# Four pairs of K tiles by seven products in some gate chunks, and a seven-product block prepared in another order

## The chip, the cores and the metric

The kernel runs on one core of a Trainium2 chip. The metric is the device time of one execution in microseconds (us). The engines are named as the profile names them: PE (TensorE, matrix products), PEld (its weight loads), DVE (VectorE), ACT (ScalarE), POOL (GpSimd, which here mostly issues DMAs) and SP (SyncE, which issues most DMAs). Each engine takes its instructions strictly in the order in which they stand in its own program.

## The reference, cut to what matters

Two layers act on a residual stream of 256 tokens by 2048 features: an SSD (Mamba-2) mixer in the first, differential attention in the second, and behind each a SwiGLU feed-forward stage. The change is in the two feed-forward stages alone:

```python
def swiglu(h, w_gate, w_up, w_down):
    return (jax.nn.silu(h @ w_gate) * (h @ w_up)) @ w_down
# h: 256 x 2048; w_gate, w_up: 2048 x 5632; w_down: 5632 x 2048, all float32
```

## The kernel before

**Products.** Every float32 operand is split into a rounded part "hi" and the remainder "lo", both in the format that PE reads, and a product of two tiles is three matmuls (hi by hi, hi by lo, lo by hi), each with 512 columns. Weights arrive by DMA as raw float32 blocks. ACT makes hi as a rounded copy (line 133) and DVE makes lo by a subtraction (line 134); the pair is called a prep. Four buffers of hi and four of lo rotate, so the hi of one prep must wait until PE has done with the prep four places earlier.

**Pairs.** `pair` (line 218) makes two neighbouring output chunks of 512 columns for both halves of the tokens (128 rows each) at once. It walks over blocks, and each block is one pair of K tiles: two K tiles by two chunks of weights, 128 x 2048 numbers. An ordinary block takes eight products (24 matmuls) and one prep. A block whose number is in the list `seven` is done by Winograd's form of Strassen's scheme with seven products (21 matmuls): sums of weight tiles stand against sums ("forms") of the activation tiles. For it the weights need a sum of two quarters that a DMA on the POOL queue adds in memory (line 247), a prep of three quarters, three additions on DVE (lines 261 to 263) and a second prep of four quarters, so it takes two hi and two lo buffers. The forms of an activation pair are made by `make_form` (line 822) from the split activations, each in one of four buffers of 128 x 1024 numbers ("xr").

**Order.** Each feed-forward stage has three parts (`PARTS`). In a part, for each pair of chunks, the gate pair is followed by the up pair, and behind the chunks of a part stand the pairs of the down projection that use them. With eight blocks in a gate or up pair, blocks 2, 4 and 6 are done by seven. The part numbers below are 1 to 3; parts 2 and 3 have two gate and two up pairs each (chunks 2 and 3, 4 and 5; 6 and 7, 8 and 9). The forms of blocks 2, 4 and 6 are kept in DRAM, since their buffers serve the down projection's forms at the end of a part, and are read back over the POOL queue (line 927) when parts 2 and 3 begin. Work put off with `later(k, ...)` is emitted k half-blocks on: so, within the second gate pair of a part, the transposes and splits of the activations of the up pair before it ("act pieces", lines 284 and 285) and a form for the down projection. A scheduler then sets the order of each engine's instructions. Five raw buffers take turns, and SP and POOL queue their DMAs ahead as buffers come free.

Of the kernel before, what the change touches and what calls it, by code (L numbers as in the profile page):

```python
# [16 lines left out]
P = 128  # L17
# [15 lines left out]
SEVEN = (2, 4, 6)  # L33

# [7 lines left out]
def trunk_kernel(ctx, tc, x_rows, x_cols, vec_cols, vec64, post_rows, lam_rows,  # L42
# [177 lines left out]
    def pair(blocks, stat, seven, form, done):  # L220
# [20 lines left out]
        for kp, src in enumerate(blocks):  # L241
# [17 lines left out]
            hi, lo = prep(raw[:, 1:4])  # L259

            nc.vector.tensor_tensor(raw[:, 2], raw[:, 2], raw[:, 0], op=ALU.add)
            nc.vector.tensor_tensor(raw[:, 3], raw[:, 3], raw[:, 2], op=ALU.add)
            nc.vector.tensor_tensor(raw[:, 1], raw[:, 2], raw[:, 1], op=ALU.subtract)  # L263
            sh, sl = prep(raw)
            mm("p1", stat(kp, 0, 0), hi[:, 1], lo[:, 1], last)
            mm((0, 0), stat(kp, 1, 0), hi[:, 2], lo[:, 2], False)
            mm((0, 1), form(kp, 3), hi[:, 0], lo[:, 0], False)
            tick()
            mm("p6", form(kp, 2), sh[:, 2], sl[:, 2], last)
            mm("p5", form(kp, 0), sh[:, 1], sl[:, 1], last)  # L270
            mm("p7", form(kp, 1), sh[:, 0], sl[:, 0], last)
            mm((1, 0), stat(kp, 1, 1), sh[:, 3], sl[:, 3], False)
# [547 lines left out]
    def make_form(dct, key, stat, t512, keep=None):  # L820
# [3 lines left out]
        for t in range(NT):  # L824
            for j in range(2):
                hi, lo = stat(key, j, t)
                nc.vector.tensor_tensor(xf[:, t, j], hi.bitcast(F32), lo.bitcast(F32), op=ALU.add)
# [30 lines left out]
    def ffn(wg, wu, wd, step, final):  # L858
# [17 lines left out]
        def kg_stat(kg, j, t):  # L876
            hi, lo = lookup(acts, (t, kg // 2))
            return hi[:, kg % 2 * 2 + j], lo[:, kg % 2 * 2 + j]
# [258 lines left out]
```

## Time and profile before

| what | value |
|---|---|
| median of 3 runs (lowest, highest) | 2540.77 us (2540.26, 2540.88) |
| the profiled execution: its time, the span of its instructions | 2539.5 us, 2537.7 us |
| PE busy | 2517.8 us, 99% |
| DVE busy | 1902.6 us, 75% |
| ACT busy | 1364.7 us, 54% |
| POOL busy | 222.4 us, 9% |
| granted TensorE clock, mean | 0.998 |

PE is busy nearly throughout, but that is a mean over stages, and PE's share says nothing on how little ahead of it the engines are that feed it. For this the timeline of DVE and ACT is set against PE's at the blocks in question: what matters is when the lo of a block ends and when PE first needs it.

### The profile page before, as it was taken

To read this page: it belongs to the slowest core of one execution; us is meant where nothing else is said; L and a number is where in the kernel's file an instruction comes from. 1 tells how busy PE (TensorE), PEld (TensorE's weight loads), DVE (VectorE), ACT (ScalarE), POOL (GpSimd) and SP (SyncE) were. 2 spreads that over 40 slices of the span, in tenths; PEclk is the share of its full clock that TensorE was granted. 3 is DMA by queue.
4 is the path that set the end of the run, shared out by engine and by line. 5 is a ranking of instruction groups with operands and counts; after the bars stand their busy time and mean duration, and the time that the engine had idled before them with its cause. 6 is when DMAs were issued, how large, how long until landed. Compare 5 with 4: busy or idle time off the path is not lost.

```text
span 2537.7 us, 31211 instructions
## 1 busy us (share of the span) xinstructions
PE 2517.8 (99%) x11866; PEld 2072.2 (82%) x11866; DVE 1902.6 (75%) x2274; ACT 1364.7 (54%) x1655; POOL 222.4 (9%) x214
## 2 busy tenths in 40 slices
PE   9999999999999999999999999999999999999998
PEld 8877888788888888888888888887888888888886
DVE  6777547777687888977887765566688889878985
ACT  5767556666565454544454654455655454535453
POOL 0111000110110000001001100001100000010002
PEclk9999999999999999999999999999999999999999
DMA  7555555455776776778677544544666966786673
GB/s 287 190 169 182 189 191 198 166 183 177 254 260 210 253 238 210 236 231 243 210 237 246 189 150 166 183 151 156 241 223 201 294 216 208 235 262 213 205 252 146
DMA packets 141366, 536.16 MB, mean 211 GB/s; under 512 B 14176, under 2 KB 30880, under 8 KB 114208
## 3 DMA queue, kind: packets, MB, share of 16 engines
q1 hardware_dynamic: 125584, 502.91, 57.3%
q0 software_dynamic: 15264, 30.94, 6.5%
q8 instruction: 93, 1.52, 0.2%
q14 instruction: 57, 0.47, 0.0%
q10 hardware_dynamic: 368, 0.32, 0.0%
HBM read 516.22 MB, written 17.89 MB: 210 GB/s over the span
## 4 chain that ended last, share of the span: by engine, by line
PE 93%; DVE 2%; ACT 1%; issue 1%; DMA 1%; POOL 0%; SPq 0%; DVEq 0%; ACTq 0%; POOLq 0%
PE acc L238 38%; PE acc L187 34%; PE cp L238 8%; PE acc L212 5%; PE acc L214 2%; DVE lo L134 1%; PE sc L1013 1%; DMA mt<-acum_d 1%; PE pt_f L291 1%; ACT hi L133 1%; PE py L568 1%; PE ptx L661 0%; PE po L1049 0%; PE pc L475 0%; PE pp L1040 0%
## 5 line engine op out<-in xcount | busy, mean ns | idle before, releaser
L134 DVE TENSOR_TENSOR lo<-raw,hi 128x2048 fp32r<-128x2048 f32 (+2 forms) x451 | 848.6, 1888 | 362.4 <-ACT hi L133 353.2
L133 ACT CAST hi<-raw 128x2048 fp32r<-128x2048 f32 (+2 forms) x451 | 699.8, 1557 | 593.9 <-DVE raw L263 195.4
L238 PE MATMUL acc<-hi,xT 128*128 128x512 f32 x1840 | 589.2, 390 | 0.0
L187 PE MATMUL acc<-hi,xT 128*128 128x512 f32 x1792 | 588.9, 399 | 0.0
L238 PEld LDWEIGHTS acc<-hi,xT 128*128 128x128 f32 x1840 | 345.3, 188 | 71.5
L187 PEld LDWEIGHTS acc<-hi,xT 128*128 128x128 f32 x1792 | 335.9, 188 | 73.4 <-issue 4.9
L238 PE MATMUL acc<-lo,xT 128*128 128x512 f32 x920 | 358.1, 389 | 0.0
L187 PE MATMUL acc<-lo,xT 128*128 128x512 f32 x896 | 352.1, 393 | 1.1 <-DVE lo L134 1.1
L133 ACT CAST hi<-rawm 128x2048 fp32r<-128x2048 f32 (+1 forms) x115 | 207.8, 1807 | 173.4 <-DVE rawm L263 108.3
L134 DVE TENSOR_TENSOR lo<-rawm,hi 128x2048 fp32r<-128x2048 f32 (+1 forms) x115 | 248.0, 2157 | 69.9 <-ACT hi L133 66.1
L238 PEld LDWEIGHTS acc<-lo,xT 128*128 128x128 f32 x920 | 172.7, 188 | 35.5
L187 PEld LDWEIGHTS acc<-lo,xT 128*128 128x128 f32 x896 | 169.0, 189 | 38.0 <-DVE lo L134 3.6
L238 PE MATMUL acc<-hi,ah_f 128*128 128x512 f32 x468 | 183.1, 391 | 0.0
L238 PE MATMUL acc<-hi,al_f 128*128 128x512 f32 x468 | 182.1, 389 | 0.0
L238 PE MATMUL acc<-lo,ah_f 128*128 128x512 f32 x468 | 182.1, 389 | 0.0
L212 PE MATMUL acc<-xT,hi 128*128 128x512 f32 x512 | 179.8, 397 | 0.0
L238 PE MATMUL cp<-hi,ff 128*128 128x512 f32 x468 | 156.9, 389 | 0.0
L214 PE MATMUL acc<-xT,lo 128*128 128x256 f32 x512 | 142.6, 280 | 0.0
L138 DVE SCALAR_TENSOR_TENSOR lo<-raw,cols,hi 128x512 fp32r<-128x512 f32 x128 | 92.5, 767 | 57.2 <-ACT hi L137 56.9
L137 ACT ACTIVATE hi<-raw,cols 128x512 fp32r<-128x512 f32 x128 | 84.8, 715 | 58.9 <-PE acc L187 41.4
L212 PEld LDWEIGHTS acc<-xT,hi 128*128 128x128 f32 x512 | 96.1, 188 | 22.6
L238 PEld LDWEIGHTS acc<-hi,al_f 128*128 128x128 f32 x468 | 87.8, 188 | 18.4
(279 smaller groups left out, 3470.4 us busy)
## 6 DMA issues: line engine op xcount, KB each, us to landing
raw<-in_w_zxbc_dram SPq DMA_DIRECT2D x77, 1024.0 KB, 4.8
raw<-in_w_d_dram SPq DMA_DIRECT2D x98, 512.0 KB, 5.9
raw<-in_w_g_dram SPq DMA_DIRECT2D x96, 512.0 KB, 5.9
raw<-in_w_u_dram SPq DMA_DIRECT2D x96, 512.0 KB, 5.8
raw<-in_w_qkv_dram SPq DMA_DIRECT2D x48, 1024.0 KB, 4.8
raw<-in_w_so_dram SPq DMA_DIRECT2D x32, 1024.0 KB, 4.8
rawm<-in_w_g_dram SPq DMA_DIRECT2D x64, 512.0 KB, 5.8
rawm<-in_w_u_dram SPq DMA_DIRECT2D x64, 512.0 KB, 6.0
```

What stands on the lines that cost most here:

```text
L133: nc.scalar.copy(hi, raw)
L134: nc.vector.tensor_tensor(lo, raw, hi.bitcast(F32), op=ALU.subtract)
L137: nc.scalar.activation(hi[:, j], raw[:, j], AF.Copy, scale=scale[j])
L138: nc.vector.scalar_tensor_tensor(lo[:, j], raw[:, j], scale[j], hi[:, j].bitcast(F32), op0=ALU.mult, op1=ALU.subtract)
L187: nc.tensor.matmul(acc[t], a, b[:, j], start=(i == 0 and j == 0 and q == 0), stop=(i == last and j == 1 and q == 2))
L212: nc.tensor.matmul(acc[ct], hi[:, j, cs], x.rearrange("p a s -> p (a s)"), start=(i == 0 and j == 0), stop=False)
L214: nc.tensor.matmul(acc[ct][:, :S], lo[:, j, cs], x[:, 0], start=False, stop=(i == last and j == 1))
L238: nc.tensor.matmul(acc[k], a, b, start=first and q == 0, stop=last and q == 2)
L291: nc.tensor.transpose(pt[:, j], src[:, j * P:(j + 1) * P], ident)
L568: nc.tensor.matmul(py[e * 64:(e + 1) * 64, a], xd[c][:, 2 * a + e], mts[c][:, 2 * a + e], start=True, stop=True)
L1013: nc.tensor.matmul(sc[c][:, h], qT[cp, h % 2, ts], kT[cp, h % 2, :nk * P], start=True, stop=True)
```

## The change

A fourth block, block 3, is done by seven products in the gate pairs of parts 2 and 3 (four pairs in each layer), so that there blocks 2, 3 and 4 are sevens one behind the other, then an ordinary block 5, then block 6. The up pairs, part 1 and the down pairs keep their lists. Block 3 needs its own form, which is made and kept beside the others (the order of making is now 3, 2, 4, 6) and read back with them. The read-backs of 4 and 6 are put off by one and by five half-blocks.

The seven-product block itself is also written anew, in all places where it stands (86 blocks against 78 before). Its first prep now covers all four quarters, with the DMA's sum among them, and so waits for that DMA. The second prep is taken apart: three rounded copies of one quarter each on ACT, between the three additions on DVE, and two subtractions (two quarters, then one). The product of the DMA's sum moves from the second half of the block to its first. `make_form` takes two additions of 256 columns in place of four of 128, and one put-off form moves from six half-blocks to eight.

```diff
+SEVEN_G = (2, 3, 4, 6)
+
+SEVEN_F = (3, 2, 4, 6)
...
             last = kp == seven[-1]
-            hi, lo = prep(raw[:, 1:4])
-
+            hi, lo = prep(raw)
+            sh = hl[0].tile([P, 3, 512], F32R, tag="hi", name=f"sh{seq[0]}")
+            sl = hl[0].tile([P, 3, 512], F32R, tag="lo", name=f"sl{seq[0]}")
             nc.vector.tensor_tensor(raw[:, 2], raw[:, 2], raw[:, 0], op=ALU.add)
+            nc.scalar.copy(sh[:, 1], raw[:, 2])
+            nc.vector.tensor_tensor(raw[:, 1], raw[:, 2], raw[:, 1], op=ALU.subtract)
+            nc.scalar.copy(sh[:, 0], raw[:, 1])
             nc.vector.tensor_tensor(raw[:, 3], raw[:, 3], raw[:, 2], op=ALU.add)
-            nc.vector.tensor_tensor(raw[:, 1], raw[:, 2], raw[:, 1], op=ALU.subtract)
-            sh, sl = prep(raw)
-            mm("p1", stat(kp, 0, 0), hi[:, 1], lo[:, 1], last)
-            mm((0, 0), stat(kp, 1, 0), hi[:, 2], lo[:, 2], False)
-            mm((0, 1), form(kp, 3), hi[:, 0], lo[:, 0], False)
+            nc.scalar.copy(sh[:, 2], raw[:, 3])
+            nc.vector.tensor_tensor(sl[:, 0:2], raw[:, 1:3], sh[:, 0:2].bitcast(F32), op=ALU.subtract)
+            nc.vector.tensor_tensor(sl[:, 2], raw[:, 3], sh[:, 2].bitcast(F32), op=ALU.subtract)
+            mm("p1", stat(kp, 0, 0), hi[:, 2], lo[:, 2], last)
+            mm((0, 0), stat(kp, 1, 0), hi[:, 3], lo[:, 3], False)
+            mm((0, 1), form(kp, 3), hi[:, 1], lo[:, 1], False)
+            mm("p7", form(kp, 1), hi[:, 0], lo[:, 0], last)
             tick()
-            mm("p6", form(kp, 2), sh[:, 2], sl[:, 2], last)
-            mm("p5", form(kp, 0), sh[:, 1], sl[:, 1], last)
-            mm("p7", form(kp, 1), sh[:, 0], sl[:, 0], last)
-            mm((1, 0), stat(kp, 1, 1), sh[:, 3], sl[:, 3], False)
+            mm("p6", form(kp, 2), sh[:, 1], sl[:, 1], last)
+            mm("p5", form(kp, 0), sh[:, 0], sl[:, 0], last)
+            mm((1, 0), stat(kp, 1, 1), sh[:, 2], sl[:, 2], False)
...
-            for j in range(2):
-                hi, lo = stat(key, j, t)
-                nc.vector.tensor_tensor(xf[:, t, j], hi.bitcast(F32), lo.bitcast(F32), op=ALU.add)
+            hi, lo = stat(key, t)
+            nc.vector.tensor_tensor(xf[:, t], hi.bitcast(F32), lo.bitcast(F32), op=ALU.add)
...
-        for k, kp in enumerate(SEVEN):
+        for k, kp in enumerate(SEVEN_F):
...
-                for kp in SEVEN:
+                def reload(kp):
                     forms[kp] = xr_tile("ff", (P, 4, 2, P), F32R)
                     nc.gpsimd.dma_start(forms[kp].rearrange("p f h q -> p (f h q)"), keep[kp])
+                forms.clear()
+                for k, kp in zip((0, 0, 1, 5), SEVEN_F):
+                    if k:
+                        later(k, lambda kp=kp: reload(kp))
+                    else:
+                        reload(kp)
...
-                        form_later(6, two[0][0])
-                    pair(twos(wg, c), kp_stat, SEVEN, form, g_done(c // 2))
+                        form_later(8, two[0][0])
+                    pair(twos(wg, c), kp_stat, SEVEN_G if pi else SEVEN, form, g_done(c // 2))
```

The engines' orders follow from the scheduler. Three places matter below. In the rows, "hi" and "lo" are the parts of a first prep (or, before, of either prep), "sh" and "sl" those of the second one in the changed kernel, "raw" and "rawm" the weight blocks, "ff" a form; the number behind the name tells buffers apart.

ACT, second gate pair of part 2 in the first feed-forward stage, from block 2 on, before:

```order
L133 CAST hi282_8336<-raw_8325 128x2048
L284 CAST ff_8375<-f_8366 128x4x128
L133 CAST hi283_8381<-rawm_8378 128x2048
L133 CAST hi284_8413<-raw_8409 128x1536
L133 CAST hi285_8420<-raw_8409 128x2048
L133 CAST hi286_8448<-raw_8445 128x2048
L133 CAST hi287_8480<-rawm_8476 128x1536
L133 CAST hi288_8487<-rawm_8476 128x2048
```

The same engine and place in the changed kernel:

```order
L269 CAST sh267_8391<-raw_8383 128x512
L137 CAST hi267_8430<-rawm_8426 128x2048
L271 CAST sh267_8391<-raw_8383 128x512
L273 CAST sh267_8391<-raw_8383 128x512
L269 CAST sh268_8434<-rawm_8426 128x512
L137 CAST hi268_8480<-raw_8476 128x2048
L271 CAST sh268_8434<-rawm_8426 128x512
L273 CAST sh268_8434<-rawm_8426 128x512
L295 CAST ff_8473<-f_8466 128x4x128
L269 CAST sh269_8484<-raw_8476 128x512
L137 CAST hi269_8518<-raw_8515 128x2048
L271 CAST sh269_8484<-raw_8476 128x512
```

Where one cast of four quarters stood for the second prep, three casts of one quarter stand now, and the whole cast of the next block's weights has come between the first and the second of them. So it is in 70 of the 86 sevens; in 12 the three stand together, and in 4 the next block's cast stands behind the second.

DVE at the same place, before (blocks 4 and 5, then the first lo of block 6):

```order
L134 TENSOR_TENSOR lo284_8414<-raw_8409,hi284_8413 128x1536
L261 TENSOR_TENSOR raw_8409<-raw_8409 128x512
L262 TENSOR_TENSOR raw_8409<-raw_8409 128x512
L263 TENSOR_TENSOR raw_8409<-raw_8409 128x512
L134 TENSOR_TENSOR lo285_8421<-raw_8409,hi285_8420 128x2048
L134 TENSOR_TENSOR lo286_8449<-raw_8445,hi286_8448 128x2048
L134 TENSOR_TENSOR lo287_8481<-rawm_8476,hi287_8480 128x1536
```

And now (block 3, then the first lo of block 4):

```order
L138 TENSOR_TENSOR lo267_8431<-rawm_8426,hi267_8430 128x2048
L268 TENSOR_TENSOR rawm_8426<-rawm_8426 128x512
L270 TENSOR_TENSOR rawm_8426<-rawm_8426 128x512
L272 TENSOR_TENSOR rawm_8426<-rawm_8426 128x512
L274 TENSOR_TENSOR sl268_8435<-rawm_8426,sh268_8434 128x1024
L275 TENSOR_TENSOR sl268_8435<-rawm_8426,sh268_8434 128x512
L138 TENSOR_TENSOR lo268_8481<-raw_8476,hi268_8480 128x2048
```

The subtraction of two quarters (line 274) stands behind ACT's second copy (line 271), and the next block's lo stands behind both subtractions; the ordinary block that lay between two sevens is gone here.

ACT in the first gate pair of part 2, blocks 2 and 3, in the changed kernel:

```order
L137 CAST hi250_7747<-rawm_7743 128x2048
L269 CAST sh251_7751<-rawm_7743 128x512
L271 CAST sh251_7751<-rawm_7743 128x512
L137 CAST hi251_7792<-raw_7788 128x2048
L273 CAST sh251_7751<-rawm_7743 128x512
L269 CAST sh252_7796<-raw_7788 128x512
L271 CAST sh252_7796<-raw_7788 128x512
L273 CAST sh252_7796<-raw_7788 128x512
L137 CAST hi252_7831<-rawm_7827 128x2048
```

Here, in the first two sevens of the pair, no cast of the next block stands ahead of the second copy.

More of the change, by code (lines that the diff above doesn't have):

```diff
@@ L874, in kp_stat, with kp_both, kg_both @@
             return x_stat(2 * kp + j, t)
-        def kg_stat(kg, j, t):
+        def kp_both(kp, t):
+            sl = slice(t * P, (t + 1) * P)
+            ks = slice(kp % 2 * 2, kp % 2 * 2 + 2)
+            return xT_hi[kp // 2][:, ks, sl], xT_lo[kp // 2][:, ks, sl]
+        def kg_both(kg, t):
             hi, lo = lookup(acts, (t, kg // 2))
-            return hi[:, kg % 2 * 2 + j], lo[:, kg % 2 * 2 + j]
+            return hi[:, kg % 2 * 2:kg % 2 * 2 + 2], lo[:, kg % 2 * 2:kg % 2 * 2 + 2]
         def form(kp, f):
@@ L911, in ffn @@
                 nc.sync.dma_start(xr_d[t][h].rearrange("p (e k) -> p e k", e=2), xr_of[(t, h)])
-        for k, kp in enumerate(SEVEN):
+        for k, kp in enumerate(SEVEN_F):
             keep[kp] = dramp.tile([P, 8 * P], F32, name=f"form{step}_{kp}")
-            later(1 + 3 * k, lambda kp=kp: make_form(forms, kp, kp_stat, t512, keep[kp]))
+            later(1 + 3 * k, lambda kp=kp: make_form(forms, kp, kp_both, t512, keep[kp]))
         mv([wu[10, k] for k in range(4)], u_stat, u_evac, LAG2)
         def form_later(k, kg):
-            later(k, lambda: make_form(dforms, kg, kg_stat, t512))
+            later(k, lambda: make_form(dforms, kg, kg_both, t512))
         md = [dramp.tile([P, D], F32, name=f"md{step}_{t}") for t in range(NT)]
```

## The prediction

> **What bounds the kernel now.** The page comes first: its busy shares and the last two lines on the chain of waits.
>
> ```profile
> PE 2517.8 (99%) x11866; PEld 2072.2 (82%) x11866; DVE 1902.6 (75%) x2274; ACT 1364.7 (54%) x1655; POOL 222.4 (9%) x214
> PE 93%; DVE 2%; ACT 1%; issue 1%; DMA 1%; POOL 0%; SPq 0%; DVEq 0%; ACTq 0%; POOLq 0%
> ```
>
> By these PE bounds all, and fewer matmuls would be less time. But the shares are means. So the second view is busy time by stretches, for the eight gate pairs that the change touches, in pairs of lines: the first and the second gate pair of part 2, then of part 3, then the same in the second layer (columns: stretch; its length; PE, PEld, DVE, ACT, POOL busy; granted clock; DMA share; GB/s).
>
> ```profile
> 898.10:939.50 41.40, 41.40 (x184) 34.28 (x183) 33.73 (x29) 20.05 (x13) 1.73 (x2) 1.00 0.75 235
> 980.90:1024.40 43.50, 43.45 (x199) 35.62 (x198) 38.71 (x45) 22.16 (x18) 2.58 (x3) 1.00 0.59 184
> 1150.90:1192.30 41.40, 41.40 (x184) 34.31 (x183) 30.99 (x25) 19.93 (x12) 5.79 (x7) 1.00 0.80 235
> 1233.60:1277.20 43.60, 43.58 (x200) 35.67 (x199) 38.81 (x45) 21.91 (x17) 2.59 (x3) 1.00 0.61 191
> 2010.40:2051.60 41.20, 41.20 (x183) 34.15 (x182) 33.52 (x28) 19.54 (x12) 2.64 (x3) 1.00 0.77 245
> 2092.90:2136.40 43.50, 43.49 (x199) 35.65 (x198) 38.72 (x45) 21.04 (x17) 2.62 (x3) 1.00 0.61 195
> 2263.10:2304.40 41.30, 41.30 (x184) 34.20 (x183) 30.41 (x26) 18.92 (x12) 6.18 (x7) 1.00 0.81 236
> 2345.60:2389.10 43.50, 43.49 (x199) 35.66 (x198) 38.71 (x45) 20.72 (x17) 2.62 (x3) 1.00 0.61 196
> ```
>
> The second pairs ("heavy", 43.5 us) carry 16 transposes, the act pieces and a form besides, and DVE works 38.7 us of 43.5; in the first ("light", 41.3 us) it works 30 to 34. The third view, the timeline of DVE and of PE in the first heavy pair, tells what DVE does with the rest (blocks 4, 5 and 6):
>
> ```profile
> 999.55 1.75 DVE L134 TENSOR_TENSOR lo<-raw,hi 128x1536 fp32r<-128x1536 f32 x1
> 1001.34 0.69 DVE L261 TENSOR_TENSOR raw<-raw 128x512 f32<-128x512 f32 x1
> 1002.07 0.69 DVE L262 TENSOR_TENSOR raw<-raw 128x512 f32<-128x512 f32 x1
> 1002.67 0.69 DVE L263 TENSOR_TENSOR raw<-raw 128x512 f32<-128x512 f32 x1
> 1005.47 4.49 DVE L134 TENSOR_TENSOR lo<-raw,hi 128x2048 fp32r<-128x2048 f32 x2 [2.11 <-ACT hi L133]
> 1009.88 1.75 DVE L134 TENSOR_TENSOR lo<-rawm,hi 128x1536 fp32r<-128x1536 f32 x1
> ...
> 1015.80 2.29 DVE L134 TENSOR_TENSOR lo<-rawm,hi 128x2048 fp32r<-128x2048 f32 x1 [2.11 <-ACT hi L133]
> 1018.01 2.28 DVE L134 TENSOR_TENSOR lo<-raw,hi 128x2048 fp32r<-128x2048 f32 x1
> ```
>
> ```profile
> 1004.63 0.39 PE L238 MATMUL acc<-hi,xT 128*128 128x512 f32 x1
> ...
> 1006.44 0.39 PE L238 MATMUL acc<-hi,xT 128*128 128x512 f32 x1
> ...
> 1007.82 0.50 PE L238 MATMUL cp<-lo,ff 128*128 128x512 f32 x1
> ...
> 1018.14 0.50 PE L238 MATMUL cp<-lo,ff 128*128 128x512 f32 x1
> ```
>
> Matmuls start 1.81/8 = 0.227 us apart. In a seven DVE subtracts, adds three times, then stands idle for 2.11 us until ACT has cast the sums. From block 4's first lo (999.55) to block 6's (1009.88) are 10.33 us; PE needs 24 + 21 = 45 matmuls for such two, 10.2 us. So DVE and ACT already set the pace here, as a loop with a wait in it. PE takes block 4's second lo at 1007.82, 0.06 us after DVE has ended it (1005.47 + 2.29), and block 6's at 1018.14, 0.05 us after its end: there is no lead left.
>
> **The change, part by part.** The sum is made against the profiled execution (2539.5 us, a span of 2537.7 and 1.8 around it), and its difference put on the median, 2540.77, which lies 1.3 us higher.
>
> *Matmuls.* Eight gate pairs lose three each: 8 x 3 x 0.227 = 5.4 us less on PE, 0.68 a pair, where PE sets the end. Nothing else on PE changes in number.
>
> *The loop of a seven, anew.* Its pieces need ACT's pace and some durations by shape:
>
> ```profile
> 1013.00 0.69 DVE L263 TENSOR_TENSOR rawm<-rawm 128x512 f32<-128x512 f32 x1
> ```
>
> ```profile
> 1013.85 1.91 ACT L133 CAST hi<-rawm 128x2048 fp32r<-128x2048 f32 x1 [5.22 <-DVE rawm L263]
> 1015.67 1.91 ACT L133 CAST hi<-raw 128x2048 fp32r<-128x2048 f32 x1
> 1017.48 0.58 ACT L276 COPY s<-cp 128x512 f32<-128x512 f32 x1
> 1017.95 1.91 ACT L133 CAST hi<-rawm 128x2048 fp32r<-128x2048 f32 x1
> ```
>
> ```profile
> L134 DVE TENSOR_TENSOR lo<-raw,hi 128x2048 fp32r<-128x2048 f32 x241 | 551.1, 2293 | 246.9 <-ACT hi L133 246.2
> L134 DVE TENSOR_TENSOR lo<-raw,hi 128x1536 fp32r<-128x1536 f32 x50 | 87.6, 1751 | 18.9 <-ACT hi L133 18.9
> L261 DVE TENSOR_TENSOR raw<-raw 128x512 f32<-128x512 f32 x50 | 34.5, 689 | 1.3
> ```
>
> A cast of four quarters holds ACT for 1.82 us, one of a quarter for 0.47 (start to start) and ends after 0.58. A lo of four quarters holds DVE for 2.21 (1015.80 to 1018.01). The subtraction of two quarters has no row; half way from 0.69 (one, taken as the addition) to 1.75 (three) it is 1.22. DVE's next one starts 0.07 ahead of an end if it waits for nothing, and ACT starts 0.16 behind DVE's end (1013.85 against 1013.00 + 0.69). In the order shown for the heavy pair the loop is: lo 2.29 + 0.04, first addition 0.69, to ACT 0.16, first copy 0.47, the next block's cast 1.82, second copy 0.58, to DVE 0.03, subtractions 1.15 + 0.61: 7.84 us from lo to next lo. DVE is idle in it for some 1.9. Before, a seven took 10.33 - 2.21 = 8.12, so the rewriting alone is worth 0.28 a seven.
>
> *Heavy pairs.* From block 2's first lo to block 7's there were three sevens and two ordinary blocks: 3 x 8.12 + 2 x 2.21 = 28.78 us. Now there are four and one: 4 x 7.84 + 2.21 = 33.57, or 4.8 more. PE needs only 4 x 4.77 + 5.45 = 24.5 for these, has no lead to spend (0.05 us), and waits; its own three matmuls fewer count for nothing here. 4 pairs x 4.8 = 19.2 us. Bounds: if the cast between the copies cost nothing, the loop is 6.0 and blocks 3 and 4 lose 1.25 each, +1.8 a pair after the saved 0.68; if each of blocks 3, 4 and 6 also waited a further 1 us for the added DMA's sum, +7.8. I take 4.8, since the order shows the cast there.
>
> *Light pairs.* Here there is a lead, as DVE's lo and PE's first use of it in block 2's second half show (part 2, then part 3):
>
> ```profile
> 906.58 2.29 DVE L134 TENSOR_TENSOR lo<-rawm,hi 128x2048 fp32r<-128x2048 f32 x1 [2.11 <-ACT hi L133]
> 1158.02 2.29 DVE L134 TENSOR_TENSOR lo<-raw,hi 128x2048 fp32r<-128x2048 f32 x1 [2.11 <-ACT hi L133]
> ```
>
> ```profile
> 912.40 0.39 PE L238 MATMUL cp<-hi,ff 128*128 128x512 f32 x1
> ...
> 1166.73 0.39 PE L238 MATMUL cp<-hi,ff 128*128 128x512 f32 x1
> ```
>
> The leads are 3.5 and 6.4 us. Blocks 3 and 4 spend 2 x (7.84 - 4.77) = 6.1. In part 3 that just fits. In part 2 the order shows no cast ahead of the second copy in blocks 2 and 3, which brings block 2 some 2 to 3 us forward, so that it nearly fits too. I book waits of 0.7, which eat the 0.68 saved: 0 for the four pairs, between -0.7 (no wait) and +2 each.
>
> *The first prep's wait for the DMA's sum.* It covers four quarters now, so it waits for the sum, and ACT's act pieces and the next copies stand behind it. Where the sum lands early this is free; part 3's down pair is where it does not:
>
> ```profile
> raw<-in_w_d_dram POOLq DMA_DIRECT2D x14, 256.0 KB, 7.2
> ```
>
> ```profile
> 1325.46 0.87 POOL L247 DMA_DIRECT2D raw<-in_w_d_dram  x1 [34.28 <-DVE sx L896]
> ```
>
> ```profile
> 1326.12 1.48 ACT L133 CAST hi<-raw 128x1536 fp32r<-128x1536 f32 x1 [5.06 <-DMA raw<-in_w_d_dram]
> ```
>
> ```profile
> 1332.72 1.75 DVE L134 TENSOR_TENSOR lo<-raw,hi 128x1536 fp32r<-128x1536 f32 x1
> ```
>
> Issue and cast are 0.7 us apart, and the median landing is 7.2 us behind the issue: the cast moves from 1326.1 to about 1332.7 and ends at 1334.6. But DVE came to its lo only at 1332.7, so 1.9 us of it show, less what PE's lead hides: +1 in each layer, +2 in all, between 0 and 4 each. [...]
>
> *The rest.* One more form a layer is made, kept and read back twice. DVE and ACT make it in the part where unit 10's products run and nothing waits for it; without that cover its eight steps, none longer than the 0.69 us of line 261, would be up to 5.5 us a layer. The read-backs of 4 and 6 move behind a sum of the gate pair on POOL's queue, tens of us ahead of their blocks (block 6 starts 3 x 5.45 + 3 x 4.77 = 30.7 us into a pair, block 4 some 20). Booked at 0.
>
> Sum: 19.2 + 0 + 2 = 21.2 us: **2562 us**, slower by 0.8%.
>
> **The rivals.**
>
> *A, faster: DVE's lead is enough and only the matmuls count.* 2540.8 - 5.4 = 2535.4 us. PE's 99% speaks for it; the 0.05 us at 1018.14 against it. It decides if the new loop takes at most 4.8 us a seven, which its DVE work alone (6.0) exceeds. 5 in 100, three of them over the line that a measurement of this kernel can tell from no change, 0.2%.
>
> *B, ACT's cast does not hold DVE up.* The heavy pairs then lose 1.8 each, the light ones win 0.7, the down pairs lose 1: 7.2 - 2.8 + 2, or about 2547 us. For it speaks that ACT is busy 51% there; against it that engines take their work in order. 12 in 100.
>
> *C, the DMA's sums set the pace.* The cast that stands between the copies is the next seven's, and it waits for that block's sum. If each of the eight gate pairs loses 1 us more by it, and the down pairs of parts 2 and 3 3 to 4 us instead of 1 in all, that is 8 + 7 more: 2577 us. For it speak the landing of 7.2 us and three sevens in a row; against it that the sum of block 3 is asked for a block ahead. 18 in 100.
>
> *D, the clock falls.* The waits come to several us within 30 us. Were PE granted half the clock from block 2 on, 129 matmuls would take 58.6 us in a heavy pair where the loop gives 33.6: 25 more in each, 2662 us. All rows above show 1.00, the waits at 1007.82 and 1018.14 among them. 2 in 100. [...]
>
> **How the numbers follow.** The forecast has 63 in 100, and 2554 to 2570 as its own range (the heavy pairs by 3.5 to 6, the light ones by 0 to 1). To leave out no more than two in ten, the range goes down to B's edge, 2547, and up to C, 2578. Faster 0.03 (A), the same 0.03 (A's rest and B's edge), slower 0.94.
>
> **What would show it.** Heavy pairs of 48 us with light ones still at 41; in them DVE waiting some 1.9 us for ACT's quarter copies ahead of line 274, three times a pair, and PE waiting for line 274's and line 138's results in blocks 3, 4 and 6. If light and heavy pairs are 0.7 us shorter, A is right; if DVE is idle nowhere ahead of line 274, B; if ACT's casts at line 137 wait for POOL's DMAs in the gate pairs, C. A new bound elsewhere, in the up pairs above all, would make the forecast wrong.

## The result: 26.8 us slower, and the profile after

The changed kernel takes 2567.29 us (median of 4 runs, 2566.15 to 2574.41), the kernel before 2540.52 us beside it (4 runs): a ratio of 1.0113, 95% interval 1.0101 to 1.0125. It is slower by 1.1%; 2562 had been forecast. The profiled execution took 2566.15 us, with a span of 2564.4 and a mean granted clock of 0.997.

The page's busy row:

```profile
PE 2524.7 (98%) x11842; PEld 2066.9 (81%) x11842; DVE 1941.9 (76%) x2370; ACT 1397.6 (54%) x1837; POOL 239.2 (9%) x226
```

PE has 24 matmuls fewer, and is busy 7 us longer: a share tells little here. Below are the stretches of the gate pairs, in the prediction's columns (stretch; length; PE, PEld, DVE, ACT, POOL busy; granted clock; DMA share; GB/s). First come the heavy pairs, then the light ones, then part 1's second down pair in both layers:

```profile
985.00:1032.50 47.50, 44.33 (x198) 34.96 (x196) 41.92 (x50) 24.94 (x27) 2.25 (x3) 1.00 0.61 189
1243.50:1291.00 47.50, 44.37 (x198) 34.93 (x197) 41.93 (x51) 24.99 (x27) 2.59 (x3) 1.00 0.60 183
2114.30:2162.30 48.00, 45.31 (x197) 36.26 (x196) 42.43 (x51) 25.19 (x27) 1.75 (x2) 0.96 0.59 180
2376.70:2424.20 47.50, 44.38 (x198) 34.95 (x197) 41.93 (x51) 25.05 (x27) 2.62 (x3) 1.00 0.58 185
...
902.20:943.50 41.30, 41.30 (x181) 33.62 (x180) 35.16 (x36) 22.84 (x22) 1.74 (x2) 1.00 0.77 244
1160.10:1202.00 41.90, 41.66 (x182) 33.56 (x181) 34.65 (x36) 22.72 (x22) 4.41 (x5) 1.00 0.78 230
2031.40:2072.80 41.40, 41.39 (x181) 33.62 (x180) 35.25 (x36) 22.66 (x22) 1.76 (x2) 1.00 0.78 249
2289.90:2335.20 45.30, 43.31 (x181) 34.71 (x180) 35.62 (x36) 23.49 (x23) 4.42 (x5) 0.96 0.74 214
...
868.50:902.20 33.70, 31.65 (x140) 25.89 (x140) 26.83 (x26) 16.15 (x15) 3.71 (x5) 1.00 0.79 256
1997.90:2031.40 33.50, 31.54 (x139) 25.81 (x138) 26.76 (x26) 15.98 (x15) 3.75 (x5) 1.00 0.79 254
```

In a heavy pair PE is now busy 44.3 of 47.5 us, where it was busy throughout; the rest are waits. In the light pairs it is busy nearly all the time but in the last. The down pairs were 31.3 us long and had no wait. A pair is found by its number of matmuls, and its length goes from its first weight load to 0.227 us behind the start of its last. Summed over both layers, against the trace of before:

| pairs (number) | before | after | difference, us |
|---|---|---|---|
| heavy gate pairs (4) | 43.8 | 47.5, one 48.0 | +15.3 |
| light gate pairs (4) | 41.5 | 41.4, 41.9, 41.4, 45.3 | +4.1 |
| part 1's second down pair (2) | 31.3 | 33.6 | +4.6 |
| part 3's down pair (2) | 43.95 | 45.3, 44.6 | +2.0 |
| second layer's first gate pair (1) | 41.95 | 43.2 | +1.2 |
| the other 17 | | | 0.0 |

Together 27.2; the spans differ by 26.7. Outside the pairs 1.4 are lost ahead of and between the two feed-forward stages, where the traces of the kernels below differ among each other by up to 1.9 without a pattern, and 2.0 are won at the program's end (see e8 below). So there are two kinds of place where time is lost: inside the gate pairs, and at the border between two pairs.

**Inside a heavy pair.** The timeline of DVE and then of ACT in the first one, from the end of block 3 on:

```profile
1005.65 1.23 DVE L274 TENSOR_TENSOR sl<-rawm,sh 128x1024 fp32r<-128x1024 f32 x1 [1.77 <-ACT sh L271]
1006.79 0.69 DVE L275 TENSOR_TENSOR sl<-rawm,sh 128x512 fp32r<-128x512 f32 x1
1007.39 2.29 DVE L138 TENSOR_TENSOR lo<-raw,hi 128x2048 fp32r<-128x2048 f32 x1
...
1010.19 0.69 DVE L268 TENSOR_TENSOR raw<-raw 128x512 f32<-128x512 f32 x1
...
1013.94 1.23 DVE L274 TENSOR_TENSOR sl<-raw,sh 128x1024 fp32r<-128x1024 f32 x1 [1.73 <-ACT sh L271]
...
1017.89 2.29 DVE L138 TENSOR_TENSOR lo<-rawm,hi 128x2048 fp32r<-128x2048 f32 x1
...
1025.71 2.28 DVE L138 TENSOR_TENSOR lo<-raw,hi 128x2048 fp32r<-128x2048 f32 x1
```

```profile
1010.97 0.62 ACT L269 CAST sh<-raw 128x512 fp32r<-128x512 f32 x1 [2.19 <-DVE raw L268]
1011.50 1.90 ACT L137 CAST hi<-raw 128x2048 fp32r<-128x2048 f32 x1
1013.30 0.61 ACT L271 CAST sh<-raw 128x512 fp32r<-128x512 f32 x1
```

The next block's cast (line 137, 1011.50) stands between the first and the second quarter copy, and DVE stands idle 1.73 us for the second (line 271). Block 6, from 1017.89 to 1025.71, takes 7.82 us; 7.84 had been worked out. Over the kernel, the view of waits gives:

```profile
DVE sl L274 <- ACT sh L271: 112.0, 69, 1.8
```

69 of the 86 sevens wait there, 1.6 us each.

**At the border.** The timeline at part 1's second down pair, of POOL, ACT, DVE and PE in this order, and behind it DVE's of the kernel before:

```profile
857.96 0.86 POOL L251 DMA_DIRECT2D raw<-in_w_d_dram  x1 [34.50 <-DMA rawm<-in_w_d_dram]
...
866.85 1.91 ACT L137 CAST hi<-raw 128x2048 fp32r<-128x2048 f32 x1 [6.84 <-DMA raw<-in_w_d_dram]
...
868.79 2.29 DVE L138 TENSOR_TENSOR lo<-raw,hi 128x2048 fp32r<-128x2048 f32 x1 [3.21 <-ACT hi L137]
871.00 0.68 DVE L296 TENSOR_TENSOR ff<-f,ff 128x512 fp32r<-128x512 f32 x1
871.60 0.69 DVE L731 TENSOR_TENSOR sw<-acc,sw 128x512 f32<-128x512 f32 x1
...
872.34 0.50 PE L242 MATMUL acc<-hi,ah_f 128*128 128x512 f32 x1 [2.05 <-DVE sw L731]
```

```profile
865.60 1.75 DVE L134 TENSOR_TENSOR lo<-raw,hi 128x1536 fp32r<-128x1536 f32 x1
867.27 0.68 DVE L720 TENSOR_TENSOR sw<-acc,sw 128x512 f32<-128x512 f32 x1
```

The cast of the new pair's first seven waits for the DMA's sum, which lands 8.7 us behind its issue (866.61; 7.6 us in the kernel before at this place). DVE's lo waits for the cast, and behind that lo, in DVE's order, stands line 731, which reads the accumulators of the pair before. PE needs these for its next products, and gets them 4.3 us later than before (0.5 of it had been lost earlier); 2.05 us of that show. The light pair that takes 45.3 us begins in the same way (timeline of ACT, then of DVE):

```profile
2288.76 1.91 ACT L137 CAST hi<-raw 128x2048 fp32r<-128x2048 f32 x1 [7.39 <-DMA raw<-in_w_g_dram]
```

```profile
2290.71 2.29 DVE L138 TENSOR_TENSOR lo<-raw,hi 128x2048 fp32r<-128x2048 f32 x1 [3.75 <-ACT hi L137]
2292.91 0.68 DVE L731 TENSOR_TENSOR sw<-acc,sw 128x512 f32<-128x512 f32 x1
```

**The clock.** Behind two of these waits PE ran at half rate for a few matmuls, which start 0.427 us apart instead of 0.227, eight and seven of them. The stretches view has the granted clock in its third column from the end:

```profile
2144.90:2148.30 3.40, 3.40 (x10) 2.63 (x9) 3.40 (x3) 0.61 (x1) 0.00 (x0) 0.53 0.66 228
...
2293.50:2298.40 4.90, 4.75 (x14) 3.77 (x15) 4.78 (x8) 1.84 (x3) 3.54 (x4) 0.65 1.13 271
```

15 x 0.2 = 3.0 us of the 26.7 are this.

### The profile page after: what moved, and what is told of

It reads as the page before. It is cut to its first block, busy times and chain, and to the rows that moved or that the text cites. A ratio compares the mean times of both kernels' runs of the same rounds, so it can differ in the third digit from the quotient of the medians.

```text
span 2564.4 us, 31464 instructions
## 1 busy us (share of the span) xinstructions
PE 2524.7 (98%) x11842; PEld 2066.9 (81%) x11842; DVE 1941.9 (76%) x2370; ACT 1397.6 (54%) x1837; POOL 239.2 (9%) x226
## 5 line engine op out<-in xcount | busy, mean ns | idle before, releaser
L138 DVE TENSOR_TENSOR lo<-raw,hi 128x2048 fp32r<-128x2048 f32 (+1 forms) x401 | 765.1, 1913 | 277.4 <-ACT hi L137 271.4
L137 ACT CAST hi<-raw 128x2048 fp32r<-128x2048 f32 (+1 forms) x401 | 627.8, 1567 | 397.5 <-PE acc L191 144.8
L191 PE MATMUL acc<-hi,xT 128*128 128x512 f32 x1792 | 589.4, 400 | 0.6 <-ACT hi L137 0.6
L242 PE MATMUL acc<-hi,xT 128*128 128x512 f32 x1608 | 523.7, 392 | 7.4 <-ACT hi L137 5.2
L191 PEld LDWEIGHTS acc<-hi,xT 128*128 128x128 f32 x1792 | 336.0, 188 | 73.9 <-issue 4.9
L242 PEld LDWEIGHTS acc<-hi,xT 128*128 128x128 f32 x1608 | 302.6, 188 | 71.5 <-ACT hi L137 6.5
L191 PE MATMUL acc<-lo,xT 128*128 128x512 f32 x896 | 352.4, 394 | 1.4 <-DVE lo L138 1.3
L242 PE MATMUL acc<-lo,xT 128*128 128x512 f32 x804 | 315.4, 392 | 1.4 <-DVE lo L138 1.4
L138 DVE TENSOR_TENSOR lo<-rawm,hi 128x2048 fp32r<-128x2048 f32 x87 | 199.0, 2287 | 27.6 <-ACT hi L137 26.6
L137 ACT CAST hi<-rawm 128x2048 fp32r<-128x2048 f32 x87 | 166.3, 1912 | 54.8 <-PE acc L242 22.3
L269 ACT CAST sh<-raw 128x512 fp32r<-128x512 f32 x54 | 33.6, 622 | 207.3 <-DVE raw L268 200.0
L274 DVE TENSOR_TENSOR sl<-raw,sh 128x1024 fp32r<-128x1024 f32 x54 | 66.2, 1226 | 74.1 <-ACT sh L271 73.3
L242 PE MATMUL cp<-sh,ff 128*128 128x512 f32 x344 | 122.2, 392 | 0.0
L141 ACT ACTIVATE hi<-raw,cols 128x512 fp32r<-128x512 f32 x128 | 84.8, 715 | 58.6 <-PE acc L191 41.4
```

The source lines that it names most:

```text
L137: nc.scalar.copy(hi, raw)
L138: nc.vector.tensor_tensor(lo, raw, hi.bitcast(F32), op=ALU.subtract)
L141: nc.scalar.activation(hi[:, j], raw[:, j], AF.Copy, scale=scale[j])
L191: nc.tensor.matmul(acc[t], a, b[:, j], start=(i == 0 and j == 0 and q == 0), stop=(i == last and j == 1 and q == 2))
L242: nc.tensor.matmul(acc[k], a, b, start=first and q == 0, stop=last and q == 2)
L269: nc.scalar.copy(sh[:, 1], raw[:, 2])
```

## The experiments

Two theories were to be told apart. By L (loop), ACT's cast between the copies makes a seven 7.84 us long, and the fourth seven in a row runs PE out of its lead. By S (sum), the first cast, which now waits for the DMA's sum, is late and holds up DVE's order at the borders. The rivals were that everything comes with the fourth seven, that such a seven is too much work in any order, and that the sums set the pace. The first four kernels ran beside each other (before: 2539.94 us), then the next four (before: 2540.92), then the last.

**The rewritten block alone (e1).**

```diff
-SEVEN_G = (2, 3, 4, 6)
+SEVEN_G = (2, 4, 6)
-SEVEN_F = (3, 2, 4, 6)
+SEVEN_F = (2, 4, 6)
-                for k, kp in zip((0, 0, 1, 5), SEVEN_F):
+                for k, kp in zip((0, 0, 0), SEVEN_F):
-                        form_later(8, two[0][0])
+                        form_later(6, two[0][0])
```

> The rewritten block (one cast of four quarters, a small product of the sum's quarter, three copies of a quarter) with the three sevens of before in every pair and no fourth one. Theory S, the first cast's wait: the cast of a pair's first seven waits for the DMA's sum, its lo comes late, and on DVE the end of the pair before (line 731) stands behind that lo, so PE finds its accumulators taken. Then part 1's second down pair keeps its +2.3 us a layer and part 3's down pair its +1.0, some 6.6 in all, and a gate pair whose sum lands late shows the same; heavy gate pairs are within 0.5 of 43.8. Total 2547 us (2544 to 2550). Theory F, everything comes with the fourth seven: all pairs as before, 2540.5 us (2539 to 2542).

Measured: 2558.53 us (2553.47 to 2560.27), 1.0069 (1.0054 to 1.0084). Theory F falls: without any fourth seven the block costs 18.6 us. S had the kind of place right and the size wrong by a factor of nearly three: the down pairs lose 6.4 (part 1's second), 6.1 (part 2's first) and 6.6 (part 3's) in the two layers together, the heavy gate pairs are 0.5 shorter each. In part 2's first down pair a queue of ACT's is to be seen that had not been counted (timeline of e1, ACT, then DVE):

```profile
2202.72 1.90 ACT L137 CAST hi<-raw 128x2048 fp32r<-128x2048 f32 x1 [8.84 <-DMA raw<-in_w_d_dram]
2204.52 1.55 ACT L295 CAST ah_f<-pt_f 128x512 fp32r<-128x512 f32 x3
```

```profile
2205.14 0.69 DVE L296 TENSOR_TENSOR al_f<-pt_f,ah_f 128x512 fp32r<-128x512 f32 x1 [3.97 <-ACT ah_f L295]
```

Three act pieces stand behind the waiting cast, DVE waits for them, and behind them in DVE's order stands the up pair's last product (line 913, 2205.74), which PE's next transposes need: PE waits 2.3 us there. In the changed kernel the same cast is as late, but the losses of this pair are zero there. DVE's order differs: the last product (line 913, 2208.68) stands ahead of the pieces' subtractions (2211.49). So the two halves of the change don't add up; what a late cast costs hangs on what is queued behind it.

**The old block with the fourth seven (e2).** The block of before is put back (a three-quarter cast, three additions, one cast of four quarters); lists, forms and read-backs are those of the change.

```diff
-            hi, lo = prep(raw)
+            hi, lo = prep(raw[:, 1:4])
             nc.vector.tensor_tensor(raw[:, 2], raw[:, 2], raw[:, 0], op=ALU.add)
-            nc.scalar.copy(sh[:, 1], raw[:, 2])
...
+            sh, sl = prep(raw)
```

> The block of before (a cast of three quarters ahead, then one cast of four quarters behind the three additions) with the fourth seven and its forms and read-backs as in the changed kernel. Theory L, the loop: a seven is 8.12 us in DVE's loop here against 7.84, so a heavy pair is 4 x 0.28 = 1.1 us longer than the 47.5 of the changed kernel, 48.6; light pairs 41.5 to 43; the first cast waits for no sum, so the down pairs are as before (31.3 and 43.95). Total 2540.5 + 4 x 4.8 + 4 x 0.7 = 2562.5 us (2558 to 2570). Theory S alone (the losses come from the first cast's wait and not from the loop): heavy pairs 43.1, light 40.8, total 2536 us.

Measured: 2576.34 us (2574.32 to 2577.13), 1.0142 (1.0126 to 1.0157). Heavy pairs take 51.2 to 52.3, light ones 43.4 in part 2 and 41.55 in part 3, all down pairs are within 0.2 of before. That the borders are clean here and the heavy pairs are longer still is what L says and S alone does not. Two loops in a row in the first heavy pair, on DVE's timeline:

```profile
999.40 2.29 DVE L138 TENSOR_TENSOR lo<-raw,hi 128x2048 fp32r<-128x2048 f32 x1 [0.63 <-ACT hi L137]
...
1007.51 2.29 DVE L138 TENSOR_TENSOR lo<-rawm,hi 128x2048 fp32r<-128x2048 f32 x1 [2.10 <-ACT hi L137]
...
1013.04 0.69 DVE L289 TENSOR_TENSOR ff<-f,ff 128x512 fp32r<-128x512 f32 x1 [0.84 <-ACT ff L288]
...
1016.94 4.49 DVE L138 TENSOR_TENSOR lo<-raw,hi 128x2048 fp32r<-128x2048 f32 x2 [2.01 <-ACT hi L137]
```

The loop is 8.11 us, as worked out, and 9.43 where a form's subtraction stands in it. A heavy pair was underestimated by some 3 us: this form, and 4 to 10 matmuls at half rate behind waits of 2.5 and 3.2 us (0.8 to 2 us). So the rewritten block is better than the old one for sevens in a row.

**The cast ahead of the copies (e3).** Loads and cast of block k + 1 are written ahead of block k's additions, and block k's copies are told to stand behind that cast:

```diff
+            raw, hi, lo = subtract(kp)
+            fetch(kp + 1)
...
+            with tc.issue_after(ready[kp + 1][3].ins):
+                nc.vector.tensor_tensor(raw[:, 2], raw[:, 2], raw[:, 0], op=ALU.add)
+                nc.scalar.copy(sh[:, 1], raw[:, 2])
+                nc.vector.tensor_tensor(raw[:, 1], raw[:, 2], raw[:, 1], op=ALU.subtract)
+                nc.scalar.copy(sh[:, 0], raw[:, 1])
+                nc.vector.tensor_tensor(raw[:, 3], raw[:, 3], raw[:, 2], op=ALU.add)
+                nc.scalar.copy(sh[:, 2], raw[:, 3])
```

`fetch` issues a block's loads, the DMA's sum and the cast (line 258), and `ready[kp + 1][3]` is that cast; `subtract` makes the lo (line 264). So the loads, the sum and the turn of the hi buffers move with the cast; this run does not part them from ACT's order.

> The changed kernel with ACT's order set by hand: the next block's cast of four quarters is issued ahead of this block's three copies of a quarter instead of between the first and the second. Nothing else. Theory L, the cast between the copies holds DVE up: the loop falls from 7.84 to some 6.0 us (2.25 lo, 2.0 additions, 1.75 subtractions), DVE waits nowhere for line 271's copy any more (112 us in 69 waits before), heavy pairs fall from 47.5 to 44.0 (43.1 to 45), light ones are 41; the down pairs keep their 4.6 + 2.0. Total 2567.3 - 14 - 1 = 2552 us (2547 to 2556). Rival W, a fourth seven is simply too much work for ACT and DVE, whatever the order: heavy pairs stay above 46.5 and the time above 2562. Rival C, the DMA's sums set the pace: the cast, now ahead of all copies, waits for its block's sum, and the time is 2567 or more.

Measured: 2538.61 us (2536.30 to 2541.37), 0.9994 (0.9985 to 1.0003) against before, 28.7 us less than the changed kernel, and below the range given: besides the 14.6 us of the heavy pairs, the light ones give back 5.7 and the down pairs 6.6, where 1 in all had been counted. Both rivals fall: the work is the same, and the sums are too. Heavy pairs are 43.95, light ones 41.07. The loop on DVE's timeline, from block 3's lo to block 5's:

```profile
995.48 2.29 DVE L264 TENSOR_TENSOR lo<-rawm,hi 128x2048 fp32r<-128x2048 f32 x1
...
1001.43 2.29 DVE L264 TENSOR_TENSOR lo<-raw,hi 128x2048 fp32r<-128x2048 f32 x1
...
1007.95 1.23 DVE L291 TENSOR_TENSOR sl<-raw,sh 128x1024 fp32r<-128x1024 f32 x1 [1.21 <-ACT sh L288]
...
1009.69 2.29 DVE L264 TENSOR_TENSOR lo<-raw,hi 128x2048 fp32r<-128x2048 f32 x1
```

Block 3 takes 5.95 us (6.0 had been worked out). Block 4 takes 8.26: only the next block's cast is bound to stand ahead, and the cast of block 6 still slips in between the copies, since block 5 is ordinary. So the waits for the copies don't vanish, as had been said, but fall to half, in 30 places instead of 69:

```profile
DVE sl L291 <- ACT sh L288: 56.6, 30, 5.8
```

The down pairs were to keep their 6.6 us, and lost all of it, though the cast still waits for the sum. A row of POOL's timeline says why:

```profile
855.40 0.86 POOL L253 DMA_DIRECT2D raw<-in_w_d_dram  x1 [33.27 <-DVE lo L264]
```

DVE is through with the pair before sooner, its buffer is free sooner, and the sum is asked for at 855.40 instead of 857.96; the cast starts at 864.40. So e3 does not separate L from S at the borders. The next one does.

**The summed quarter apart (e4).** A seven's first cast and its lo cover quarters 1 to 3; quarter 0 follows behind the first addition.

```diff
-            hi, lo = prep(raw)
+            nc.scalar.copy(hi[:, 1:4], raw[:, 1:4])
+            nc.vector.tensor_tensor(lo[:, 1:4], raw[:, 1:4], hi[:, 1:4].bitcast(F32), op=ALU.subtract)
             nc.vector.tensor_tensor(raw[:, 2], raw[:, 2], raw[:, 0], op=ALU.add)
+            nc.scalar.copy(hi[:, 0], raw[:, 0])
+            nc.vector.tensor_tensor(lo[:, 0], raw[:, 0], hi[:, 0].bitcast(F32), op=ALU.subtract)
             nc.scalar.copy(sh[:, 1], raw[:, 2])
```

> The changed kernel with a seven's first cast cut in two: quarters 1 to 3, which need no sum, are cast and subtracted first, and quarter 0, which the DMA adds into, after the first addition. Theory S: the lo no longer waits for the sum, DVE comes to the end of the pair before in time, and the second down pair of part 1 is 31.3 again (33.6), part 3's down pair 44.0 (44.6 to 45.3), the first matmuls of a light gate pair wait for nothing; heavy pairs are still 46 to 48, since the fourth seven's loop is there. Total 2567.3 - 4.6 - 2 - 4 = 2556.5 us (2552 to 2560). Rival: the end of the pair before is late for another reason (DVE's own order, its load), and the time is 2566 to 2569 with part 1's second down pair at 33.6.

Measured: 2552.99 us (2551.71 to 2554.59), 1.0051 (1.0034 to 1.0068). S holds at the borders: part 1's second down pair is 31.28 again in both layers, the light pairs are 41.05 without a wait, and the second layer's first gate pair is 41.95 again. The heavy pairs, though, are 45.5 and not 46 to 48; one of their four waits, that of 1.5 us for line 138, is gone, and the next is 0.4 shorter; why was not settled. And part 3's down pair got worse, by 3.7 and 5.7 us against before (timeline of e4 in the first layer, ACT, then DVE):

```profile
1335.87 0.62 ACT L274 CAST hi<-raw 128x512 fp32r<-128x512 f32 x1 [7.00 <-DMA raw<-in_w_d_dram]
1336.40 1.55 ACT L302 CAST ah_f<-pt_f 128x512 fp32r<-128x512 f32 x3
```

```profile
1337.01 0.69 DVE L303 TENSOR_TENSOR al_f<-pt_f,ah_f 128x512 fp32r<-128x512 f32 x1 [7.22 <-ACT ah_f L302]
```

Here the small cast waits 7.0 us for the sum with three act pieces queued behind it, and DVE stands still for 7.2 us. It is the wait of e1 again, moved to a smaller instruction: what counts is not how much the cast covers but what stands behind it.

**Three sevens with the cast ahead (e5).** As e3, with e1's lists.

> The kernel with the cast ahead of the copies (e3), but with the three sevens of before in every pair: what the fourth seven is worth once ACT's order is right. Theory L: a loop of 6.0 us is still 1.25 more than PE's 4.77, so two sevens in a row spend lead; in a light pair, which has lead, the fourth is worth what it saves, 0.4 to 0.68, in a heavy one it costs 0.66 (43.95 with it, 43.27 without). So light pairs 41.48, heavy 43.3, and the total 2538.6 + 4 x 0.41 - 4 x 0.66 = 2537.6 us (2535.5 to 2540). Rival V, the fourth seven brings its 0.68 us in each of the eight pairs as soon as the cast is out of the way: without it 2538.6 + 5.4 = 2544 us.

Measured: 2540.70 us (2538.27 to 2543.35), 0.9999 (0.9990 to 1.0008), 0.7 above the range given. By the pairs theory L is met: heavy 43.3 (43.95 with the fourth), light 41.48 (41.07 with it). So rival V falls: in e3's order the fourth seven wins 0.4 us in a light pair and costs 0.7 in a heavy one. The excess over 2537.6 is part 1's second down pair, 0.65 and 0.37 longer, and the program's end, 2.7 us longer than in e3 as in the kernel before; less the 1.7 us that e3 loses at the second layer's first gate pair, 2539.6 comes out.

**Both, cast ahead and summed quarter apart (e6).** e3's order with e4's cast; four sevens.

> Cast ahead of the copies, and a seven's first cast without the summed quarter, which is cast behind the first addition; four sevens in the gate pairs as in the changed kernel. Theory S: what is left of the first cast's wait in e3, PE's 1.7 us at the start of the second layer's feed-forward block (lo ahead of line 897's product on DVE), goes too; the two halves of the cast cost ACT 0.1 and DVE 0.08 a seven. Total 2538.6 - 1.7 = 2537 us (2534 to 2538.5), with no wait of over 0.5 us there, and down pairs at 31.3 and 43.95. Rival: with the small cast of quarter 0 standing between the casts ahead and the copies, ACT waits for sums with everything behind it; then the light pairs lose their 0.4 and part 3's down pair 2 to 4, and the time is 2542 or more.

Measured: 2535.27 us (2534.13 to 2536.09), 0.9979 (0.9970 to 0.9987). No border shows a wait: the second layer's first gate pair is back at 41.97 (43.64 in e3), and part 3's down pair, which e4 had made worse, at 43.95. The heavy pairs are 43.3, as with three sevens, the light ones 41.25. The rival, that the small cast gives the gain back, holds only for 0.2 us in each light pair.

**Cast ahead, the fourth seven in light pairs only (e7), and all three together (e8).**

```diff
-                    pair(twos(wg, c), kp_stat, SEVEN_G if pi else SEVEN, form, g_done(c // 2))
+                    pair(twos(wg, c), kp_stat, SEVEN_G if pi and c != part[-2] else SEVEN, form, g_done(c // 2))
```

> Cast ahead of the copies, and the fourth seven only in the light gate pairs (the first of parts 2 and 3); the heavy ones have three. By theory L this takes the better of e3 and e5 in each kind of pair: light 41.07, heavy 43.3, total 2538.6 - 4 x 0.66 = 2536.0 us (2533.5 to 2538). Rival: the heavy pairs are as long without the fourth seven as with it (43.95), and the time is that of e3, 2538.6.

> All three together: cast ahead, summed quarter apart, the fourth seven in light gate pairs only. Theories L and S add up: 2536.0 - 1.7 = 2534.3 us (2532 to 2536.5), 6.2 us less than the kernel of before. Rival: the summed quarter's own cast eats the light pairs' 0.41 and 2536 to 2538 comes out.

Measured: e7 2535.88 us (2533.71 to 2539.56), 0.9981 (0.9972 to 0.9990); e8 2534.79 us (2533.71 to 2535.45), 0.9975 (0.9966 to 0.9985). Both came as worked out. e8 is the quickest of all, 6.1 us below before and 32 below the change, though e6, with all eight fourth sevens, cannot be told from it. Where each kernel lost or won, in us over both layers against the trace of before:

| kernel | heavy (4) | light (4) | part 1's 2nd down (2) | part 3's down (2) | other pairs | program's end | median |
|---|---|---|---|---|---|---|---|
| the change | +15.3 | +4.1 | +4.6 | +2.0 | +1.2 | -2.0 | 2567.3 |
| e1 block alone | -2.1 | +1.4 | +6.4 | +6.6 | +7.2 | 0.0 | 2558.5 |
| e2 old block, fourth seven | +31.3 | +3.9 | 0.0 | +0.4 | +0.5 | -2.7 | 2576.3 |
| e3 cast ahead | +0.8 | -1.6 | 0.0 | 0.0 | +1.7 | -2.7 | 2538.6 |
| e4 summed quarter apart | +7.0 | -1.7 | 0.0 | +9.4 | +0.8 | -2.7 | 2553.0 |
| e5 cast ahead, three sevens | -2.1 | 0.0 | +1.0 | 0.0 | 0.0 | 0.0 | 2540.7 |
| e6 cast ahead, quarter apart | -2.0 | -0.9 | 0.0 | 0.0 | 0.0 | -2.7 | 2535.3 |
| e7 cast ahead, light only | -2.1 | -1.7 | +1.0 | 0.0 | +1.9 | -2.7 | 2535.9 |
| e8 all three | -2.1 | -0.9 | 0.0 | 0.0 | 0.0 | -2.7 | 2534.8 |

"Program's end" is what follows the last pair. It is 2.7 us shorter in each kernel with a fourth seven, though PE's work there is the same: POOL's closing DRAIN instruction takes 8.23 us in the kernel before, in e1 and in e5, where POOL issues 106 DMAs, and 4.6 to 4.9 us in the others, where it issues 114 or 118 (the change loses 0.6 of the 2.7 again ahead of it). No run tries the reason. So e8's lead is not all won in the blocks: in the traces it is 4.1 us, of which 3.0 lie in the pairs and 2.7 at the end, less 1.5 elsewhere. By their pairs e5 and e7 are alike (-1.0 and -0.8), and 2.7 of the 4.8 us between their medians stand at the end.

**Waits of a set length (e9).** e8, and in block 5 of each up pair DVE repeats a quarter's subtraction:

```diff
+            if kp == 5:
+                for _ in range(again):      # 10 to 13, by pair
+                    nc.vector.tensor_tensor(lo[:, 2], raw[:, 2], hi[:, 2].bitcast(F32), op=ALU.subtract)
```

> The kernel of e8 with one wait of a set length put into each of its ten up pairs, to see what a wait alone does to TensorE's clock: in block 5 DVE repeats one quarter's subtraction (the same result again) 10 to 13 times, so that PE runs out of its lead once and idles some 2.0, 2.2, 2.2, 3.2, 3.2, 3.4, 3.4, 3.4, 4.4 and 4.7 us, by a replay of the durations of the traces. Theory H, seen in the changed kernel and in e1 and e2: behind a wait of over some 2 us the matmuls start 0.43 us apart for 2 to 3.5 us, but not behind each; then most of the waits of 3 us and more are followed by 5 to 16 slow matmuls, some of those of 2 us too, and the time is 2534.8 + 30 for the waits + 6 to 12 for the clock, 2571 to 2577 us. [...]

Measured: 2580.66 us (one run), with ten waits of 1.75 to 4.37 us from one matmul's start to the next, and a further one of 1.63. In the view by stretches, a wait of 3.2 us and one of 2.0 us, each with the stretch behind it:

```profile
1239.00:1242.00 3.00, 0.27 (x2) 0.00 (x0) 3.00 (x6) 0.00 (x0) 0.00 (x0) 1.00 0.56 180
1242.00:1246.00 4.00, 3.95 (x11) 3.11 (x12) 3.39 (x3) 0.00 (x0) 0.00 (x0) 0.60 0.99 344
...
978.90:980.90 2.00, 0.44 (x2) 0.01 (x1) 2.00 (x5) 0.00 (x0) 0.00 (x0) 1.00 0.33 86
980.90:985.00 4.10, 4.07 (x18) 3.38 (x19) 3.97 (x4) 1.47 (x1) 0.00 (x0) 1.00 0.88 303
```

All seven waits of 2.9 us and more are followed by 5 to 7 matmuls at half rate, none of the four of 2.0 and less. So the idling itself does it, in a pair that has no such stretch otherwise. The time lies 3.7 us above the forecast's upper end; in the up pairs alone 42 us were lost, of which the ten waits that stand there are 27.3 and the 45 slow matmuls 9.0. The rest was not taken apart.

## Why the prediction was right, and where it was not

- **The sign and the size:** 21.2 us forecast, 26.8 found. The bound was read rightly: not PE's 99%, but the missing lead at 1018.14, with DVE and ACT in a loop that includes a wait. That the sum came so near is in part luck: the heavy pairs' term was 3.9 too large, the light pairs and the borders together 9.9 too small, and 2.0 won at the program's end were not foreseen.
- **The loop of a seven:** 7.84 worked out, 7.82 found, with its cause at the place named. e3 bears the term out: with the cast out from between, block 3 takes 5.95, the 6.0 of the bound.
- **Heavy pairs:** the mechanism was right, the term too large: 4.8 forecast for each, 3.7 found (one 4.3, with half-rate matmuls). The sum took four sevens with a wait of 1.9 us each. But in block 2 DVE has six of the form's steps and two act pieces to do (992.88 to 997.70), and does them while it would wait for ACT, so only three of the four sevens wait (1.73 to 1.77 us, in the first heavy pair): from block 2's first lo to block 7's it needed 32.39 us before and needs 35.08, 2.7 more and not 4.8; block 2's own lo also starts 2.2 us later in the pair. And that PE's "own three matmuls fewer count for nothing" was not so: a pair grew by 3.7 net of the 0.68 saved, so by waits of 4.4.
- **Light pairs:** 0 forecast, +4.1 found. Three of them differ by -0.1, -0.1 and +0.4: the waits do eat what the matmuls save. The fourth lost 3.8, mostly at its border and by the clock and not in the loop, so it belongs to the next step.
- **The first prep's wait for the sum** is the step that failed. "Where the sum lands early this is free; part 3's down pair is where it does not" was tested at one pair only. That pair was right (+2 forecast, +2.0 found). But the sum is also late at part 1's second down pair (+4.6), at the second layer's first gate pair (+1.2) and at one light pair (some 2.2 of its 3.8). And of what stands behind the waiting cast, the text named ACT's pieces and copies, and not DVE's lo with the end of the pair before behind it, for which PE waits. e4 shows this cause by itself at these three places.
- **The rest at 0:** right for the forms and read-backs, as far as the pairs tell: no up pair moved. The new `make_form` stands in all these kernels and was not tried alone. The program's end, 2.0 us shorter, had no term.
- **The rivals.** A needed a loop of 4.8 and is out. B, that ACT's cast does not hold DVE up, is out as it stands, but e3 and e6 make it come true by order: heavy pairs +0.2 and -0.5. C came in part, at the borders and not in the gate pairs' loops. D came in small: 3.0 us by half-rate matmuls, not 25 a pair. (D's own sum is off: the stretch of 33.6 us holds 108 matmuls and not 129, which at the 0.427 us found behind the waits take 46.1 us, 12.5 more.)
- **The clock.** PE fell to half rate behind one wait of 2.38 us (to 2293.65) and one of 1.76 us (to 2142.72), from one matmul's start to the next. The forecast had no term for it, and the trace of before could not show it: from 700 us on no two matmuls start more than 1.08 us apart there. What the later traces tell stands in the last section.

## What to carry to other kernels

Where an engine waits for a transfer, look at what is queued behind it on each engine down to the one that sets the end, and at every place where the instruction stands, not only at the one that looks worst: at a border between two stages it can hold up the end of the stage before. When a loop over two engines turns out too slow, look at the order in which the slower partner takes its work before giving up the idea; here one cast moved ahead of a copy, with the loads that belong to it, was worth 28.7 us, and with the late sum taken out of its way 1.1% slower became 0.2% faster, nearly half of that by the program's shorter end. So a lead of a few us over a long kernel is to be looked for in the trace, stretch by stretch, before it is put down to the change. Work of another stage that fell into an idle gap cost nothing here (block 2's steps: 2.7 us more by DVE where 4.8 were forecast), so a loop's price is not to be multiplied by the number of its turns without a look at what fills them.

## What the runs showed of the hardware

Behind some waits PE's matmuls start 0.427 us apart instead of 0.227 for a while. Over the changed kernel and e1 to e9, by the distance of two matmuls' starts, 12 of 12 waits of 2.9 us and more were followed by 4 to 7 matmuls at that distance, 3 of 9 waits of 2.3 to 2.8 us were followed by some, and below that one, of 1.76 us, 3.7 us behind another of 1.55. The slow stretch began 0.4 to 2.4 us behind the wait and lasted 1.7 to 3.4 us, so such a wait cost 0.8 to 1.6 us more than itself.

The length of a wait alone does not tell which was followed. In the changed kernel the wait of 2.38 us (to 2293.65) was, and those of 2.44 us (to 872.34) and 2.35 us (to 2001.57) were not. Each heavy pair has three waits one behind the other, of 1.54 to 1.55, 1.75 to 1.77 and 0.74 us, and only in the third pair were they followed by it. That trace records a granted clock of 0.50 from 2144.68 and from 2294.87, each time for 3.413 us, and from 2557.70, at the program's end; from the first start to the second are 44 times 3.413 us, from the second to the third 77 times. Below, the trace is cut into stretches of that length (150.186 / 44 = 3.4133), counted from 2144.68: two with the wait of 2.44 us, then the one with the wait of 2.38 us and the one behind it (the columns of the stretches):

```profile
868.10:871.51 3.41, 2.19 (x10) 1.49 (x8) 2.72 (x2) 1.17 (x2) 0.00 (x0) 1.00 1.10 334
871.51:874.93 3.42, 2.59 (x11) 2.18 (x12) 3.38 (x7) 0.71 (x2) 0.00 (x0) 1.00 1.08 406
...
2291.46:2294.87 3.41, 1.42 (x6) 1.04 (x6) 3.41 (x5) 0.00 (x0) 0.98 (x2) 1.00 1.08 301
2294.87:2298.28 3.41, 3.41 (x9) 2.65 (x9) 3.29 (x5) 1.84 (x3) 2.56 (x3) 0.50 1.13 259
```

With each matmul counted as 0.227 us from its start, PE's work fills 33% of the stretch ahead of this half clock and 39% of the one ahead of the other. The wait of 2.44 us lies across two stretches, with 60% and 72%; the one of 2.35 us leaves 45% of its stretch, the least of any other between 750 and 2520 us, and the waits of the other heavy pairs leave 46 to 48%. So in this trace, with two cases, the work within such a stretch goes with the clock, and the length of one wait does not. No run shifted a wait against these stretches, so that the work decides was not shown.

The sum that a DMA adds into memory, 256 KB, landed 8.7 us behind its issue at a border (857.96 to 866.61) and 7.6 us at the same place of the kernel before, where the median of all 78 sums is 4.8 us (4.0 to 9.2). Weight loads, and from 864.38 on read-backs, are in flight beside it at the border. That these lengthen it was not tried.
